# Values of the dilated heads: from four strided token classes per chunk of four heads to copies in class order and one product for all eight

## The chip, the cores and the metric

The kernel runs on one core of one Trainium2 chip, as one launch. The metric is the time on the device in microseconds (us), as the median of several runs. The engines of a core are named as in the profile: PE (TensorE, matrix products) and PEld (its loads of the stationary operand), DVE (VectorE), ACT (ScalarE), POOL (GpSimd), and SP (SyncE), whose queue issues most transfers. They run side by side and wait for one another by semaphores. On-chip memory is SBUF; products are summed in PSUM, eight banks of 512 float32 per partition.

## The reference

One decoder layer on 512 tokens of width 1024, in float32:

```python
x = x + 1/2 * SwiGLU_1(RMSNorm(x))                 # width 2816
h = RMSNorm(x)
[qkv_A | qkv_B | gate_A | gate_B] = h @ W_in       # A: 12 heads of 64, B: 8 heads of 64
y_A = dilated window attention over three groups of four heads:
      (window 128, dilation 1), (512, 4), (2048, 16), merged by their softmax denominators
y_B = block-sparse attention (block 256), causal inside the blocks
x = x + (sigmoid(gate_A) * (y_A @ W_up_A) + sigmoid(gate_B) * (y_B @ W_up_B)) @ W_out
x = x + 1/2 * SwiGLU_2(RMSNorm(x))
return RMSNorm(x)
```

With dilation 4 or 16 a token attends only to tokens of its own class, t % 4. The eight heads of those two groups (heads 4 to 11 of A) are the dilated heads of the title.

## The kernel before

The residual stream is kept transposed, as eight tiles of 128 features by 512 tokens. Every float32 operand is split into two parts, hi and lo; a product is the sum of hi*hi, hi*lo and lo*hi, so `mac` issues three matmuls. After the first feed-forward half, `normed` leaves the normalised stream as `XN[k]`, a pair (hi, lo) of tiles [128, 512] for each k.

All weights come in one stream of tiles [128, up to 1024], in the order of their use: `fetch` loads a tile, `split` casts it to its hi part on ACT and subtracts to get the lo part on DVE (lines 182 and 183), and `weights` hands out the next tile after it has asked for the split of the one after it. The split parts have two buffers each. TensorE's instructions run in the order of the program text; the order of the other engines' is chosen by a planner when the kernel is built.

Queries and keys are projected with the weights as stationary operand and 512 tokens moving (`project`). Then `stacked` scales them by the row factor of the norm (line 460; for the dilated pairs the tokens are put in class order, with strided operands), splits them (462, 463), and sends the parts to their places with transfers on SP's queue (474 and 476). The values have tokens on the partitions: the stationary operand is a tile of 128 tokens of `XN[k]`, and the moving one is 256 columns of weights, the four heads of a chunk c:

```python
mac(ps[t // 2][:, at:at + n], [tokens(x, t, dilated) for x in XN[k]], cols(w, kk, n), ...)
```

For the chunks 1 and 2, which hold the dilated heads, `tokens` takes every fourth token (`by_class(x)[:, t]`), so 128 columns with a step of four elements, 16 bytes. A chunk has 8 x 4 steps of three matmuls, and its four sums of 256 columns share two banks; they are scaled by the row factor as a column per token (`columns`, line 257) into hi and lo parts (506, 507).

The mixers start with the list `FIRST`: pair 0 of heads (before the norm's factor is there), pairs 1 and 2, and chunk 1 of the values. `factors` computes the norm's row factor with a Newton step (230 to 234), `columns` spreads it. After that each of the four dilated heads, and each pair of the other kind, has two parts, scores and weighted sums (`dsa_scores`, `weighted`), and `blend` spreads the steps of the projections named in `BESIDE` over the steps of each part:

```python
FIRST = [("qk", 0), ("qk", 1), ("qk", 2), ("v", 1)]
BESIDE = [
    [("v", 2), ("v", 0)], [("qk", 3)],
```

`project`, `values` and `gate` take turns on four banks ("acc"). In `weighted` the transposed rows go to tiles tagged `pth` and `ptl`, three buffers each. `bias` (line 514) is POOL's only work in the mixers: slopes times distances.

Of the kernel before, what the change touches and what calls it, by code (L numbers as in the profile page):

```python
"""One core: a macaron SwiGLU pair around a gated merge of dilated window attention and MoBA.

The residual stream is kept transposed, [d_model on partitions, tokens], so that every projection
takes the weights as the stationary operand and the tokens as the moving one. A float32 operand is
split exactly into two float32r parts (hi + lo, 12 significant bits each); a product is the sum of
hi*hi, hi*lo and lo*hi, added up in float32 in PSUM. Query-key and probability-value products are
small and carry all four parts, hi and lo stacked on the partitions.

The RMSNorm's row factor is applied to the outputs of the projections that follow it, its gain to
their inputs. With MOBA_TOPK >= the number of blocks every past block is selected, so MoBA is causal  # L10
attention here. The three groups of the dilated attention are one softmax over their joint keys.
"""
# [28 lines left out]
# Heads by pairs, as they are projected: those of the dilated attention, then MoBA's.  # L41
# [3 lines left out]
def by_class(ap):  # L45
    """[P, tokens] as [P, class t % 4, t // 4]."""
    return ap.rearrange("p (i r) -> p r i", r=NT)


def slopes(n):  # L50
# [7 lines left out]
# The projections of the mixers: those before the attention, and those beside each part of it  # L58
# (scores and weighted sums of each head of the dilated attention, then of each pair of MoBA's).
FIRST = [("qk", 0), ("qk", 1), ("qk", 2), ("v", 1)]  # L60
BESIDE = [
    [("v", 2), ("v", 0)], [("qk", 3)],
# [11 lines left out]
def blend(main, side, lead=0):  # L74
    """Run a generator beside others: `lead` steps of the others, then the rest spread over those of `main`.

    Each comes with its number of steps."""
    (main, total), left = main, sum(n for _, n in side) - lead
    steps = (None for g, _ in side for _ in g)
    done = 0  # L80
    for _ in range(lead):
        next(steps, None)
    for at in range(1, total + 1):
        while done * total < left * at:
            next(steps, None)
            done += 1
        next(main, None)
    for _ in main:
        pass
    for _ in steps:  # L90
        pass
# [3 lines left out]
def decoder_layer(ctx: ExitStack, tc: tile.TileContext, xT, gains, gus, gu1, dn1, wqk, wv, wg, wup, wout, gu2, dn2, base, out):  # L95
# [20 lines left out]
    def warm_up(n):  # L116
        """Keep the tensor engine's clock up while it waits."""
        ps = bank("all")
        for _ in range(n):
            nc.tensor.matmul(ps[:, :P], ones, ones, start=True, stop=True)  # L120

# [11 lines left out]
    CHUNKS = [slice(c * P, min(c + 8, FT) * P) for c in range(0, FT, 8)]  # L133

    def mixer_tiles(what, n, *js):
        src = {"qk": lambda j: wqk[2 * n + j], "v": lambda j: wv[n, j], "g": lambda j: wg[2 * n + j]}[what]
        return [((what, n, j), src(j)) for j in js or range(2)]
# [49 lines left out]
    def weights(*key):  # L187
        """The next tile of the stream, split, with the ones after it on their way."""
# [7 lines left out]
    def mac(ps, w, x, first, last):  # L196
        """ps += w.T @ x for split operands."""
# [12 lines left out]
    def normed(i, k):  # L210
        """Tile k of the stream times the gain, split; and its part of the sum of squares."""
# [16 lines left out]
    def newton(y, z, a, out):  # L228
        """out = 1/sqrt(a): a step from the reciprocal of the table's square root."""
# [6 lines left out]
    def factors(i, ps):  # L236
        """1/rms of each token, as rows on all partitions."""
# [14 lines left out]
    def columns(row, dilated):  # L252
        """The same as columns [token of the tile, tile], tiles of 128 tokens or of a class of tokens."""
# [7 lines left out]
    def tokens(x, t, dilated):  # L261
        """Tile t of the tokens of x [P, tokens]."""
        return by_class(x)[:, t] if dilated else x[:, t * P:(t + 1) * P]

# [1 line left out]
    def first_tiles():  # L266
        """Gate and up of the first two tiles, side by side over k as x comes in."""
# [60 lines left out]
    def last_tile(A):  # L328
        """The last tile of the stream in two halves of the tokens, each followed by its part of the output."""
# [99 lines left out]
    with ExitStack() as mix:  # L429
# [15 lines left out]
        def project(t, j, which="acc"):  # L445
            """Queries (j = 0) or keys (j = 1) of a pair of heads, transposed."""
# [6 lines left out]
        def stacked(t, j, ps):  # L453
            v = tpool.tile([P, S], F32, name="qkv", tag="ssq", bufs=1)
            # The scores are kept with the sign turned, as their minimum is then the softmax's bias.
# [8 lines left out]
            # For each head: q as [hi; lo], k as [hi; hi] and [lo; lo].  # L464
# [21 lines left out]
        def values(c):  # L486
            """Values of four heads, tokens on partitions, [hi | lo] per head."""
            # Two tiles of tokens share a bank: its first product clears it for both.
            ps = [bank("acc") for _ in range(2)]
            n = 4 * HD  # L490
            dilated = c in (1, 2)
            col = R["col"][dilated]
            for half in range(2):
                w = weights("v", c, half)
                for kk in range(4):
                    k = 4 * half + kk
                    for t in range(NT):
                        at = (t % 2) * n
                        mac(ps[t // 2][:, at:at + n], [tokens(x, t, dilated) for x in XN[k]], cols(w, kk, n),
                            k == 0 and t % 2 == 0, k == KT - 1 and t % 2 == 1)  # L500
                        yield
            for t in range(NT):
                v = V[t, c] = mp.tile([P, 4 * P], F32R, name=f"v{t}_{c}", tag=f"v{t}_{c % 3}", bufs=1)
                heads = v.rearrange("p (h c) -> p h c", c=P)
                pv = ps[t // 2][:, (t % 2) * n:(t % 2 + 1) * n].rearrange("p (h c) -> p h c", c=HD)
                nc.scalar.mul(heads[:, :, :HD], pv, col[:, t:t + 1])
                nc.vector.scalar_tensor_tensor(heads[:, :, HD:], pv, col[:, t:t + 1], f32(heads[:, :, :HD]),
                                               ALU.mult, ALU.subtract)

        def bias(tag, n, *parts):  # L510
            """Slopes times distances, in [P, n]."""
# [5 lines left out]
        def row_of(row, ps, b, low, den):  # L517
            """exp(score - max) of a row of scores, with its turned maximum and its sum."""
# [3 lines left out]
        def dsa_scores(h, rows):  # L522
            """Rows of the joint softmax of head h of each of the three groups.

            The dilated groups go by the classes t % 4 of the tokens, in which all their keys lie."""
            bb = bias("biasb", 256, (BAND, sl_a[h], 0))
            bd = bias("biasd", 256, (DILATED[:, :P], sl_a[4 + h], 0), (DILATED[:, P:], sl_a[8 + h], P))
            # [low or sum, own or other, by tiles or by classes, tile]
# [5 lines left out]
            for r in range(NT):  # L534
# [5 lines left out]
                # The two parts of the keys side by side: one long product instead of two short ones.  # L540
# [13 lines left out]
            # Each order of the tokens gets the other's minima and sums: a permutation, exact as it adds zeros.  # L554
# [32 lines left out]
        def moba_scores(heads, rows):  # L587
            """Rows of the softmax of each head over all keys up to its own."""
# [16 lines left out]
        def weighted(steps, ytile, half, classes=False):  # L605
            """The rows' sums of values, transposed, into half a tile of y.

            A step is up to four blocks of the rows to transpose, and the products that they go into:
# [266 lines left out]
```

## Time and profile before

| what | us |
|---|---|
| median of 3 runs | 1162.74 |
| lowest and highest run | 1161.46, 1162.74 |
| span of the profiled execution | 1162.7 |
| PE busy | 1150.9 (99%) |
| DVE, ACT, POOL busy | 597.9, 413.5, 19.6 |

The profiled execution's time is its span, from the first to the last instruction; it stands at the median of the runs. Busy times are sums over the span. Matmuls are pipelined and a record of one lasts longer than its place in the stream, so a busy PE is not a PE at its peak: the distance from one start to the next tells the pace. The mean granted clock of PE is 0.999 of full speed.

### The profile page before, as it was taken

To read this page: it belongs to the slowest core of one execution; us is meant where nothing else is said; L and a number is where in the kernel's file an instruction comes from. 1 tells how busy PE (TensorE), PEld (TensorE's weight loads), DVE (VectorE), ACT (ScalarE), POOL (GpSimd) and SP (SyncE) were. 2 spreads that over 40 slices of the span, in tenths; PEclk is the share of its full clock that TensorE was granted. 3 is DMA by queue.
4 is the path that set the end of the run, shared out by engine and by line. 5 is a ranking of instruction groups with operands and counts; after the bars stand their busy time and mean duration, and the time that the engine had idled before them with its cause. 6 is when DMAs were issued, how large, how long until landed. Compare 5 with 4: busy or idle time off the path is not lost.

```text
span 1162.7 us, 13714 instructions
## 1 busy us (share of the span) xinstructions
PE 1150.9 (99%) x5418; PEld 966.8 (83%) x5418; DVE 597.9 (51%) x975; ACT 413.5 (36%) x641; POOL 19.6 (2%) x35
## 2 busy tenths in 40 slices
PE   8999999999999999999999999999999999999997
PEld 7888888888888899888998888888888888888886
DVE  5745444433333633777677667754744444433223
ACT  5433233222222323544454445433422323322222
POOL 0000000000000100000000000000000000000001
PEclk9999999999999999999999999999999999999999
DMA  5232232233233461446364222332233233233321
GB/s 200 93 107 91 95 105 91 94 97 100 87 99 122 140 173 55 128 127 164 111 162 127 74 64 82 110 99 99 91 96 104 91 96 103 91 100 84 98 82 73
DMA packets 37599, 122.14 MB, mean 105 GB/s; under 512 B 4752, under 2 KB 4768, under 8 KB 37536
## 3 DMA queue, kind: packets, MB, share of 16 engines
q1 hardware_dynamic: 37072, 120.08, 34.3%
q10 hardware_dynamic: 432, 1.18, 0.3%
q8 instruction: 42, 0.69, 0.2%
q14 instruction: 21, 0.17, 0.0%
q0 software_dynamic: 32, 0.02, 0.0%
HBM read 103.44 MB, written 2.10 MB: 91 GB/s over the span
## 4 chain that ended last, share of the span: by engine, by line
PE 98%; DVE 0%; DMA 0%; ACT 0%; issue 0%; DVEq 0%; POOLq 0%
PE ps_all L199 20%; PE ps_all L201 20%; PE ps_all L200 20%; PE ps_acc L199 9%; PE ps_acc L201 9%; PE ps_acc L200 9%; PE ps_all L276 2%; PE ps_out L640 2%; PE ps_att L621 1%; PE ps_att L199 1%; PE ps_att L200 1%; PE ps_att L201 1%; PE ps_att L596 1%; DMA g_sb<-in_gains_dram 0%; PE ps_att L538 0%; PE ps_att L550 0%
## 5 line engine op out<-in xcount | busy, mean ns | idle before, releaser
L182 ACT CAST whi<-raw 128x1024 fp32r<-128x1024 f32 (+2 forms) x201 | 202.8, 1010 | 562.4 <-PE ps_all L200 259.9
L183 DVE TENSOR_TENSOR wlo<-raw,whi 128x1024 fp32r<-128x1024 f32 (+2 forms) x202 | 236.2, 1170 | 174.1 <-ACT whi L182 174.0
L200 PE MATMUL ps_all<-xl,whi 128*128 128x512 f32 x672 | 261.4, 389 | 0.0
L199 PE MATMUL ps_all<-xh,whi 128*128 128x512 f32 x672 | 261.4, 389 | 0.0
L201 PE MATMUL ps_all<-xh,wlo 128*128 128x512 f32 x672 | 261.4, 389 | 0.0
L200 PEld LDWEIGHTS ps_all<-xl,whi 128*128 128x128 f32 x672 | 126.1, 188 | 26.3
L201 PEld LDWEIGHTS ps_all<-xh,wlo 128*128 128x128 f32 x672 | 126.1, 188 | 26.3
L199 PEld LDWEIGHTS ps_all<-xh,whi 128*128 128x128 f32 x672 | 126.1, 188 | 26.0
L199 PE MATMUL ps_all<-ah,whi 128*128 128x512 f32 (+1 forms) x374 | 143.1, 383 | 0.0
L200 PE MATMUL ps_all<-al,whi 128*128 128x512 f32 (+1 forms) x374 | 142.7, 382 | 0.0
L201 PE MATMUL ps_all<-ah,wlo 128*128 128x512 f32 (+1 forms) x374 | 142.7, 382 | 0.0
L199 PE MATMUL ps_acc<-xh,whi 128*128 128x512 f32 x272 | 110.2, 405 | 0.0
L201 PE MATMUL ps_acc<-xh,wlo 128*128 128x512 f32 x272 | 106.9, 393 | 0.0
L200 PE MATMUL ps_acc<-xl,whi 128*128 128x512 f32 x272 | 106.4, 391 | 0.0
L290 DVE TENSOR_TENSOR fu<-ps_all,rrow 128x512 f32<-128x512 f32 x44 | 30.4, 691 | 124.1 <-PE ps_all L201 124.1
L200 PEld LDWEIGHTS ps_all<-al,whi 128*128 128x128 f32 x374 | 70.2, 188 | 15.2
L201 PEld LDWEIGHTS ps_all<-ah,wlo 128*128 128x128 f32 x374 | 70.2, 188 | 15.1
L199 PEld LDWEIGHTS ps_all<-ah,whi 128*128 128x128 f32 x374 | 70.2, 188 | 15.0
L288 DVE TENSOR_TENSOR fg<-ps_all,rrow 128x512 f32<-128x512 f32 x44 | 30.4, 691 | 79.8 <-PE ps_all L201 79.7
L201 PEld LDWEIGHTS ps_acc<-xh,wlo 128*128 128x128 f32 x272 | 51.0, 188 | 11.3
L200 PEld LDWEIGHTS ps_acc<-xl,whi 128*128 128x128 f32 x272 | 51.3, 189 | 7.4
L199 PEld LDWEIGHTS ps_acc<-xh,whi 128*128 128x128 f32 x272 | 51.3, 188 | 7.4
(158 smaller groups left out, 1321.3 us busy)
## 6 DMA issues: line engine op xcount, KB each, us to landing
raw<-in_gu_dram SPq DMA_DIRECT2D x84, 512.0 KB, 3.4
raw<-in_dn_dram SPq DMA_DIRECT2D x32, 512.0 KB, 3.5
raw<-in_wqk_dram SPq DMA_DIRECT2D x20, 512.0 KB, 3.5
ks<-qkhl SPq DMA_DIRECT2D x40, 256.0 KB, 4.9
raw<-in_wg_dram SPq DMA_DIRECT2D x16, 512.0 KB, 3.5
raw<-in_dn_dram SPq DMA_DIRECT2D x16, 384.0 KB, 3.1
raw<-in_wv_dram SPq DMA_DIRECT2D x10, 512.0 KB, 4.0
qs<-qkhl SPq DMA_DIRECT2D x40, 128.0 KB, 2.6
```

Of the source, the lines that this page charges most:

```text
L182: nc.scalar.copy(hi[:, s], raw[:, s])
L183: nc.vector.tensor_tensor(lo[:, s], raw[:, s], f32(hi[:, s]), ALU.subtract)
L199: nc.tensor.matmul(ps, wh, xh, start=first, stop=False)
L200: nc.tensor.matmul(ps, wh, xl, start=False, stop=False)
L201: nc.tensor.matmul(ps, wl, xh, start=False, stop=last)
L276: nc.tensor.matmul(ps[j], w[:, at:at + P], x, start=k == 0 and n == 0, stop=k == KT - 1 and n == 2)
L288: nc.vector.tensor_tensor(g, ps[0], R, ALU.mult)
L290: nc.vector.tensor_tensor(u, ps[1], R, ALU.mult)
L596: nc.tensor.matmul(ps[:, :n], Q[NA + h][:, i * P:(i + 1) * P], K[NA + h][:, part, :n], start=part == 0, stop=part == 1)
L621: nc.tensor.transpose(pt[:, n * P:(n + 1) * P], block, ident)
L640: nc.tensor.matmul(to(po), V[v[0], v[1] // 4][:, v[1] % 4 * P:(v[1] % 4 + 1) * P], x[:, first:first + n], start=done == 1, stop=done == 2 ...
```

## The change

The values of the eight dilated heads are no longer two chunks of four. A new part `("vd", 0)` stands right after pair 0 in `FIRST`, and `("v", 1)` and `("v", 2)` are gone from the lists. `values_by_class` takes all four "acc" banks, one for each class of tokens, and works through the eight tiles of the stream. For each, POOL copies the hi and the lo part into class order, into tiles that share the tags `pth` and `ptl` (three buffers each); the products take 128 consecutive columns of a copy as stationary operand and all eight heads' 512 columns of weights as the moving one. The weights are four tiles of two times 512 columns in place of two times two tiles of four times 256. The eviction is the same per class and chunk (`keep_values`). Comments and documentation strings are removed too.

```diff
-FIRST = [("qk", 0), ("qk", 1), ("qk", 2), ("v", 1)]
+FIRST = [("qk", 0), ("vd", 0), ("qk", 1), ("qk", 2)]
 BESIDE = [
-    [("v", 2), ("v", 0)], [("qk", 3)],
+    [("v", 0)], [("qk", 3)],
...
     def mixer_tiles(what, n, *js):
-        src = {"qk": lambda j: wqk[2 * n + j], "v": lambda j: wv[n, j], "g": lambda j: wg[2 * n + j]}[what]
-        return [((what, n, j), src(j)) for j in js or range(2)]
+        src = {"qk": lambda j: wqk[2 * n + j], "v": lambda j: wv[max(0, n - 2), j], "vd": lambda j: wvd[j], "g": lambda j: wg[2 * n + j]}[what]
+        return [((what, n, j), src(j)) for j in js or range(4 if what == "vd" else 2)]
...
         def values(c):
             ps = [bank("acc") for _ in range(2)]
             n = 4 * HD
-            dilated = c in (1, 2)
-            col = R["col"][dilated]
...
-                        mac(ps[t // 2][:, at:at + n], [tokens(x, t, dilated) for x in XN[k]], cols(w, kk, n),
+                        mac(ps[t // 2][:, at:at + n], [x[:, t * P:(t + 1) * P] for x in XN[k]], cols(w, kk, n),
...
+                keep_values(t, c, ps[t // 2][:, (t % 2) * n:(t % 2 + 1) * n], R["col"][False])
+
+        def keep_values(t, c, pv, col):
+            v = V[t, c] = mp.tile([P, 4 * P], F32R, name=f"v{t}_{c}", tag=f"v{t}_{c % 3}", bufs=1)
+            heads = v.rearrange("p (h c) -> p h c", c=P)
+            pv = pv.rearrange("p (h c) -> p h c", c=HD)
+            nc.scalar.mul(heads[:, :, :HD], pv, col[:, t:t + 1])
+            nc.vector.scalar_tensor_tensor(heads[:, :, HD:], pv, col[:, t:t + 1], f32(heads[:, :, :HD]),
+                                           ALU.mult, ALU.subtract)
+
+        def values_by_class():
+            ps = [bank("acc") for _ in range(NT)]
+            n = 8 * HD
+            for quarter in range(4):
+                w = weights("vd", 0, quarter)
+                for kk in range(2):
+                    k = 2 * quarter + kk
+                    copies = []
+                    for x, tag in zip(XN[k], ("pth", "ptl")):
+                        xc = mp2.tile([P, S], F32R, name="xc", tag=tag, bufs=3)
+                        nc.gpsimd.tensor_copy(xc.rearrange("p (r i) -> p r i", r=NT), by_class(x))
+                        copies.append(xc)
+                    for r in range(NT):
+                        mac(ps[r], [x[:, r * P:(r + 1) * P] for x in copies], cols(w, kk, n), k == 0, k == KT - 1)
+                        yield
+            for r in range(NT):
+                for c in (1, 2):
+                    keep_values(r, c, ps[r][:, (c - 1) * 4 * HD:c * 4 * HD], R["col"][True])
...
+            if what == "vd":
+                return values_by_class(), NT * KT
...
-        "wv": np.stack([_moving(v[:, c:c + 256], 4) for c in range(0, v.shape[1], 256)]),
+        "wv": np.stack([_moving(v[:, c:c + 256], 4) for c in (0, 768, 1024)]),
+        "wvd": _moving(v[:, 256:768], 2),
```

## Rows read from the trace of the kernel before

**Rows 1.** The page: busy time of each engine; chain that ended last.

```profile
PE 1150.9 (99%) x5418; PEld 966.8 (83%) x5418; DVE 597.9 (51%) x975; ACT 413.5 (36%) x641; POOL 19.6 (2%) x35
...
PE 98%; DVE 0%; DMA 0%; ACT 0%; issue 0%; DVEq 0%; POOLq 0%
```

**Rows 2.** Windows: stretch, its length, busy time (x instructions) of each engine.

```profile
372.92:384.26 11.34, 11.34 (x51) 9.39 (x50) 5.12 (x6) 4.28 (x6) 4.04 (x8) 1.00 0.54 182
384.26:406.03 21.77, 21.77 (x98) 18.07 (x96) 17.95 (x32) 7.35 (x9) 0.00 (x0) 1.00 0.52 145
406.03:452.30 46.27, 46.27 (x206) 46.27 (x206) 15.38 (x31) 12.69 (x25) 0.60 (x2) 1.00 0.46 125
```

**Rows 3.** Weight loads by form, 406 to 431 us, dilated values: total, mean.

```profile
L199 PEld LDWEIGHTS ps_acc<-whi,xh 128*128 128x128 f32 x37 | 12.2, 328 | 0.0
```

**Rows 4.** The same from 452.3 to 464 us, plain values.

```profile
L199 PEld LDWEIGHTS ps_acc<-whi,xh 128*128 128x128 f32 x32 | 6.1, 192 | 0.0
```

**Rows 5.** Timeline, TensorE, dilated and plain products: start, duration, engine.

```profile
407.08 0.39 PE L201 MATMUL ps_acc<-whi,xl 128*128 128x256 f32 x1
407.32 0.39 PE L199 MATMUL ps_acc<-whi,xh 128*128 128x256 f32 x1
...
453.70 0.28 PE L200 MATMUL ps_acc<-wlo,xh 128*128 128x256 f32 x1
453.82 0.28 PE L201 MATMUL ps_acc<-whi,xl 128*128 128x256 f32 x1
```

**Rows 6.** POOL's groups by form over the span.

```profile
L514 POOL TENSOR_SCALAR bias<-consts 128x256 f32<-128x256 f32 x4 | 1.6, 406 | 390.8 <-PE ps_att L201 375.5 <-DVE st L519 15.2
...
L371 POOL TENSOR_TENSOR yo<-yo,rrow 128x256 f32<-128x256 f32 x8 | 5.6, 729 | 499.0 <-ACT rrow L363 499.0
```

**Rows 7.** Timeline, 591 to 595 us, POOL and VectorE.

```profile
591.23 0.62 POOL L514 TENSOR_SCALAR bias<-consts 128x512 f32<-128x512 f32 x1 [100.61 <-DVE low L519]
...
593.11 1.23 DVE L183 TENSOR_TENSOR wlo<-raw,whi 128x1024 fp32r<-128x1024 f32 x1
...
593.26 1.55 POOL L514 TENSOR_SCALAR bias<-consts 128x512 f32<-128x512 f32 x1 [1.42 <-DVE low L519]
...
594.25 1.10 DVE L463 TENSOR_TENSOR qkhl<-qkv,qkhl 128x512 fp32r<-128x512 f32 x1
```

**Rows 8.** Timeline of VectorE, 387 to 400 us.

```profile
387.19 3.35 DVE L231 RECIPROCAL root<-root 128x512 f32<-128x512 f32 x1 [0.90 <-ACT root L230]
390.58 0.69 DVE L232 SCALAR_TENSOR_TENSOR step<-root 128x512 f32<-128x512 f32 x1
...
394.40 0.69 DVE L460 SCALAR_TENSOR_TENSOR qkv<-ps_att,rrow 128x512 f32<-128x512 f32 x1
...
397.76 1.23 DVE L183 TENSOR_TENSOR wlo<-raw,whi 128x1024 fp32r<-128x1024 f32 x1
398.89 0.70 DVE L463 TENSOR_TENSOR qkhl<-qkv,qkhl 128x512 fp32r<-128x512 f32 x1
399.62 1.05 DVE L460 SCALAR_TENSOR_TENSOR qkv<-ps_acc,rrow 128x512 f32<-128x512 f32 x1
```

**Rows 9.** Timeline, keys 409 to 417, first head 468 to 472 us.

```profile
409.04 3.15 SPq L476 DMA_DIRECT2D ks<-qkhl  x4
...
415.97 0.62 ACT L462 CAST qkhl<-qkv 128x512 fp32r<-128x512 f32 x1 [4.44 <-DMA ks<-qkhl]
...
468.74 2.13 DVE L585 TENSOR_SCALAR prow<-prow,jf 128x128 f32<-128x128 f32 x8
...
471.50 0.60 PE L621 MATMUL ps_att<-ident,prow 128*128 128x128 f32 x4
```

**Rows 10.** Timeline of TensorE at the start.

```profile
7.12 2.08 PE L276 MATMUL ps_all<-xh,whi 128*128 128x512 f32 x4 [2.28 <-ACT xh L215]
8.99 1.91 PE L276 MATMUL ps_all<-xh,wlo 128*128 128x512 f32 x4
10.70 1.91 PE L276 MATMUL ps_all<-xl,whi 128*128 128x512 f32 x4
```

More of the change, by code (lines that the diff above doesn't have):

```diff
@@ L94, in decoder_layer @@
 @with_exitstack
-def decoder_layer(ctx: ExitStack, tc: tile.TileContext, xT, gains, gus, gu1, dn1, wqk, wv, wg, wup, wout, gu2, dn2, base, out):
+def decoder_layer(ctx: ExitStack, tc: tile.TileContext, xT, gains, gus, gu1, dn1, wqk, wv, wvd, wg, wup, wout, gu2, dn2, base, out):
     nc = tc.nc
@@ L502, in values @@
             for t in range(NT):
[L503 to L508, printed above, removed]
+                keep_values(t, c, ps[t // 2][:, (t % 2) * n:(t % 2 + 1) * n], R["col"][False])
[24 more added lines that the diff above has]
+                    keep_values(r, c, ps[r][:, (c - 1) * 4 * HD:c * 4 * HD], R["col"][True])
         def bias(tag, n, *parts):
```

## The prediction, made before the changed kernel was run

> **What bounds the kernel now.** I read the page's busy shares and its chain first, then the chain's stages by windows, and inside the stage that the diff touches the weight loads, the start times of the products and the other engines' queues. TensorE is the bound throughout: it is busy 99% of the span and is 98% of the chain that ended last [rows 1]. So a change is worth what it takes out of TensorE's stream, less whatever TensorE must newly wait for.
>
> The windows cut the start of the mixers into the first pair of heads (from 372.92), the pairs 1 and 2 (from 384.26), and the dilated values with twelve score products among them (from 406.03) [rows 2]. In the second of these, 96 products of 512 columns (x98 with the two cut at the edges) take 21.77 us: 0.227 us each. In the third, 192 products of only 256 columns and the twelve scores take 46.27 us, and the weight loads are busy for all of it, not 83% as in the stage before: there the loads set the pace, not the products. The loads that take every fourth token as stationary column are 328 ns [rows 3]; the same loads for the undilated values are 192 ns [rows 4]. The starts agree: 0.24 us from one dilated product to the next, 0.12 us from one plain product to the next, both with 256 columns [rows 5].
>
> **The change, part by part.**
>
> *Removed.* The projections v1 and v2 with their 2 x 32 x 3 = 192 products: 46.27 us [rows 2] less the twelve scores, at the 0.12 us of an unstrided product of 256 columns [rows 5] 1.4 us, is 44.9 us, 0.234 us each.
>
> *Added on TensorE.* Four classes x eight tiles x three parts = 96 products of 512 columns on a stationary tile without a stride. A load of 192 ns hides behind a product of 0.227 us, as it does in the stage of rows 2, so the price is that row's 21.8 us. The net is -23.1 us. If the load stayed at 328 ns it would be 31.5 us; a stationary operand of the same shape without a stride is what rows 4 show, so I leave that out of the range.
>
> *Added on POOL.* Sixteen copies of 128x512, two for each tile of the stream, read with a step of four elements. POOL is otherwise nearly idle. No row shows it read with a step. Without one, and with one operand, it takes 0.41 us for 256 elements [rows 6] and 0.62 us for 512 (the slopes at 591.23 [rows 7]): 0.20 us fixed and 0.82 ns an element. What a step costs others: VectorE's 128x512 scaling rises from 0.69 to 1.05 us when its operands go by classes, 0.70 ns an element [rows 8]; TensorE's load rises by (328 - 192)/128 = 1.06 ns [rows 3, 4]. That puts a copy at 0.98 to 1.17 us; I take 1.1, of which 0.9 is reading. Bounds: 0.62 us if the step is free; and the two-operand POOL row, 0.73 us for 256 elements or 2.1 ns each [rows 6], with 1.06 ns more for the step, gives 1.8 us.
>
> *Do the copies themselves come in time?* Each pair serves 12 products, 2.72 us. Three pairs have room. They can start when the first feed-forward half has let go of its memory, near 373, and the first is wanted at 384.3; six copies (6.6 us), the eight slopes (4.0 us) and all of VectorE's work there (5.1 us) [rows 2] still end by 389, when the third pair is wanted at 389.7. The other ten start at 387.0, when the first pair is read, and the last must be there at 384.3 + 7 x 2.72 = 403.3: at up to 1.6 us a copy that holds if nothing disturbs POOL.
>
> *What disturbs it, and what it disturbs.* The slopes at 593.26 took 1.55 us instead of 0.62, while VectorE subtracted two SBUF operands (593.11 to 594.34); VectorE's next subtraction of two operands then took 1.10 us [rows 7], and 0.70 where POOL is idle [rows 8]. So POOL and a VectorE instruction with two SBUF operands take turns. VectorE has such a train just here: from 390.58 to 398.99 it steps Newton's root, splits a tile of weights, takes eight columns, splits the first queries, scales twice (from PSUM, one SBUF operand) and splits the next tile of weights [rows 8], 8.4 us with no gap worth naming. That last split is wanted when the fourth tile of the new projection begins, at 384.3 + 3 x 5.44 = 400.6; before it has 1.6 us to spare. Now the eight copies of the last four pairs fall into the train. Taking turns it ends at 390.58 + 8.4 + 8 x 0.9 - 1.2 (the two scalings run beside the copies) = 405.0, and TensorE waits 4.4 us for weights. Behind the train stand the evictions of the new sums; they are not late, as the columns come before the split. With copies of 0.62 us (0.42 of reading) the wait is 0.6 us; with 1.8 us (1.6) it is 10.0 us.
>
> A rule that speaks against the change: the Trainium skill, GPSIMD Engine Reference, section Performance pitfalls for Q7 kernels, gives 2.9 cycles an element at 1.2 GHz where the step is over 8 bytes, and 1.9 below. Rows 6 and 7 show 0.82 ns an element without a step, half of the page's lower figure, and no row here has the step. By the page a copy would be an estimated 0.20 + 1.24 = 1.44 us, the wait 7.1 us and the time 1146.7 us, where by the rows it is 4.4 us and 1144.0 us.
>
> *Evictions.* The same 16 instructions in place of 2 x 8; the next projection takes the first of the four banks at once, but that bank is closed nine products (2.0 us) before the end, and its two scalings on ScalarE and two subtractions on VectorE, half as long as the 0.70 us of 128x512 [rows 8] or a little more, overlap to about three in a row. I put 0, at most 1 us.
>
> *Order.* Between the keys of pair 1 and the first scores lay pair 2 and v1, now only pair 2, 10.9 us and three steps of v0, 1.1 us. The keys' way is the scaling 1.05, a cast 0.62, a subtraction 0.70 and the transfers, 6.9 us from issue at 409.04 to the cast that waited for them until 415.97 [rows 8, 9]: 9.5 us with the gaps, inside 12.0. The first head's scores now have v0 alone beside them, 96 products at 0.12 over 13 steps, so 0.9 us of TensorE a step, and not another 96 at 0.234; the second head has as much from its gate, 48 products of 512 columns. The rows of the first head are ready at 470.87 and transposed at 471.50 [rows 9], with v0 beside them then too; 0.6 us to spare, so 0 with up to 1 us lost.
>
> *Sum.* The profiled execution's span is 1162.7 us, and the median of the runs is 1162.74, so nothing is added for what lies around it. 1162.7 - 44.9 + 21.8 + 4.4 = **1144.0 us**.
>
> **The rivals.**
> - *Hidden* (1139 to 1141.5): copies near 0.7 us, or the split put ahead of the columns in VectorE's queue. For it: 1.6 us of slack and three buffers. Against it: rows 7 and the order of rows 8. 1139.6 us.
> - *Slow copies* (1146.5 to 1152.5): 1.4 to 1.8 us each, by the two-operand row; 7 to 10 us of waits: 1147 to 1150.
> - *The clock falls.* At the start TensorE idled 2.28 us, and its next eight products took 1.71 to 1.87 us for four, 0.43 us each, twice the later 0.227, as 1.2 GHz stands to 2.4 [rows 10]. If a wait of 4.4 us in one piece does the same, at least eight products cost 1.8 us more: 1146 us. The granted clock is 1.00 in every window of rows 2, as there is no wait in them. The Trainium skill, TensorE: Matmul & The Clock Gate, Part 1, says that an idle engine is throttled to 1.2 GHz; by it the wait would cost that much on top, if it is not broken up by work.
> - *Slower than before*: POOL's copies set the pace of the whole projection. The place is the wait of each group of products for its pair; the price is 8 x reading - 2.8, and it decides when a copy passes 3.4 us (8 x 3.2 - 2.8 = 22.8). The only row that slow per element is VectorE's reciprocal, 3.35 us for 512 and no copy; POOL's slowest row is a third of it. At 3.8 us: 1165.6 us.
> - *No change*: the loads keep their 328 ns and the wait comes on top: 1162.7 - 44.9 + 31.5 + 4.4 = 1153.7 us, still faster; only with slow copies does it reach 1160 or more. Rows 4 speak against it.
>
> **How the numbers follow.** The forecast (1141.5 to 1146.5, without a fall of the clock) has 45%, hidden copies 25%, slow copies 17%, a fallen clock 8%, slower 3%, no change 2%. A difference of 0.2%, 2.3 us, is about what these runs can tell from none. Faster 0.95, within 0.2% 0.02, slower 0.03. The range runs from 1139.0, all hidden and every small term nought, to 1152.5, copies of 1.8 us with the clock's price on top.
>
> **What would show it.** Right: no weight load of 328 ns is left; 96 products of 512 columns start 0.227 us apart except where they wait; POOL has sixteen copies of about 1.1 us, longer beside VectorE's subtractions; the longest wait of TensorE in the new projection is near its fourth tile of weights and names VectorE's split (or its copy). Wrong, if that wait is nil, if the waits stand at each pair of copies, if the loads of the copied tiles are not near 192 ns, or if the first scores wait for keys.

## The result, and the profile after

| | before | after |
|---|---|---|
| median of the runs, us | 1162.74 | 1145.30 (1144.41 to 1146.97, 4 runs) |
| ratio, 95% interval | | 0.9852 [0.9841, 0.9864] |
| span of the profiled execution, us | 1162.7 | 1144.1 |

The forecast was 1144.0 us within 1139.0 to 1152.5. Of all executions behind this text one, of 3176.71 us in the experiment e3 below, was disturbed and stands in no number. The page of the changed kernel, first the busy times, then the shares of the chain that ended last:

```profile
PE 1129.3 (99%) x5322; PEld 939.9 (82%) x5322; DVE 605.0 (53%) x975; ACT 413.0 (36%) x641; POOL 42.5 (4%) x51
...
PE 97%; DVE 2%; DMA 0%; issue 0%; ACT 0%; DVEq 0%; POOLq 0%
```

Beside [rows 1], TensorE has 96 products fewer, POOL sixteen instructions more and 23 us more of busy time, and VectorE now has 2% of the chain, where it had 0%. These 2% hold the longest wait of the new stage. The windows of the first pair and of the new projection (length, then busy time and instructions of PE, PEld, DVE, ACT and POOL, granted clock, share of the DMA engines, GB/s), and of two stretches near the projection's end:

```profile
371.63:382.98 11.35, 11.35 (x51) 9.38 (x50) 7.90 (x6) 4.19 (x6) 10.75 (x10) 1.00 0.52 169
382.98:410.64 27.66, 24.59 (x98) 18.95 (x96) 22.33 (x33) 8.72 (x14) 16.08 (x15) 0.94 0.43 122
403.40:405.00 1.60, 1.60 (x4) 1.31 (x5) 1.60 (x2) 0.33 (x1) 0.00 (x0) 0.50 0.49 142
407.00:408.00 1.00, 1.00 (x6) 0.77 (x6) 0.00 (x0) 0.00 (x0) 0.00 (x0) 1.00 1.03 254
```

The eight heads' values take 27.66 us, where the two chunks before took about 45 [rows 2]. TensorE is idle for 3.07 us of them, and for another 3 us it runs at a granted clock of 0.50. Its waits from 370 to 440 us (total, times, longest) and its weight loads in the projection:

```profile
PE ps_acc L200 <- DVE wlo L183: 2.8, 1, 2.8
PE ps_acc L199 <- DVE v L509: 0.2, 1, 0.2
```

```profile
L199 PEld LDWEIGHTS ps_acc<-whi,xc 128*128 128x128 f32 x31 | 6.2, 201 | 2.1 <-POOL xc L525 0.5
```

There is one wait worth naming, it is for VectorE's split, and the loads of the copied tiles are 201 ns and not 328 [rows 3]. TensorE's timeline at the fourth tile of weights, and after the last product (start, duration):

```profile
399.55 0.39 PE L201 MATMUL ps_acc<-whi,xc 128*128 128x512 f32 x1
400.01 0.47 PE L199 MATMUL ps_acc<-whi,xc 128*128 128x512 f32 x1
403.32 0.79 PE L200 MATMUL ps_acc<-wlo,xc 128*128 128x512 f32 x1 [2.83 <-DVE wlo L183]
403.91 0.63 PE L201 MATMUL ps_acc<-whi,xc 128*128 128x512 f32 x1
404.33 0.63 PE L199 MATMUL ps_acc<-whi,xc 128*128 128x512 f32 x1
...
406.81 0.39 PE L199 MATMUL ps_acc<-whi,xc 128*128 128x512 f32 x1
...
410.08 0.39 PE L201 MATMUL ps_acc<-whi,xc 128*128 128x512 f32 x1
410.64 0.47 PE L199 MATMUL ps_acc<-xh,whi 128*128 128x512 f32 x1 [0.17 <-DVE v L509]
```

Products start 0.23 us apart. The first product of the fourth tile needs only the hi part (`whi`) and starts 0.23 late; the second needs the lo part and starts 3.31 us after it, 3.08 late. Then products come 0.43 us apart: the eight starts from 403.32 to 406.81 take 3.49 us instead of 8 x 0.233 = 1.86, so 1.6 us go to the clock. The next projection starts 0.33 us late, for a bank. Together: 96 x 0.233 = 22.4, and 0.23 + 3.08 + 1.6 + 0.33, makes 27.6 of the 27.66 us.

The queue of VectorE before that split, and POOL's copies beside it:

```profile
389.30 1.05 DVE L232 SCALAR_TENSOR_TENSOR step<-root 128x512 f32<-128x512 f32 x1
390.38 1.47 DVE L233 TENSOR_TENSOR step<-step,mean 128x512 f32<-128x512 f32 x1
391.78 2.13 DVE L183 TENSOR_TENSOR wlo<-raw,whi 128x1024 fp32r<-128x1024 f32 x1
393.83 1.58 DVE L234 SCALAR_TENSOR_TENSOR rrow<-step,root 128x512 f32<-128x512 f32 x1
...
398.68 1.22 DVE L257 CUSTOM_DVE_ANT_0 rest<-rrow,ident 128x128 f32<-128x128 f32 x1
399.83 0.28 DVE L257 CUSTOM_DVE_ANT_0 rest<-rrow,ident 128x128 f32<-128x128 f32 x1
...
402.06 1.21 DVE L183 TENSOR_TENSOR wlo<-raw,whi 128x1024 fp32r<-128x1024 f32 x1
```

```profile
388.68 1.12 POOL L525 CAST xc<-xh 128x512 fp32r<-128x512 f32 x1 [0.38 <-PE ps_acc L200]
389.74 1.56 POOL L525 CAST xc<-xl 128x512 fp32r<-128x512 f32 x1
...
392.77 2.10 POOL L525 CAST xc<-xl 128x512 fp32r<-128x512 f32 x1
...
398.54 1.19 POOL L525 CAST xc<-xl 128x512 fp32r<-128x512 f32 x1
```

The train runs from 389.30 to the split's end at 403.27, 13.97 us, where it had 8.4 before [rows 8]. The split of the third tile took 2.13 us instead of 1.22, the Newton step on line 234 1.58 instead of 0.68. The copies stop at 399.73, and from there on VectorE's column takes 0.28 us, where the one before took 1.22. POOL stretches with it: 1.10 to 1.12 us for a copy beside VectorE's reciprocal, which reads one operand, and up to 2.10 beside its split of two SBUF operands.

ScalarE shows a second link that the forecast did not have:

```profile
398.30 0.62 ACT L462 CAST qkhl<-qkv 128x512 fp32r<-128x512 f32 x1 [8.41 <-DVE qkv L460]
398.82 1.04 ACT L182 CAST whi<-raw 128x1024 fp32r<-128x1024 f32 x1
```

The cast that makes the fourth tile's hi part stands in ScalarE's queue behind pair 0's cast, and that one waited 8.41 us for VectorE's scaling. So both parts of the fourth tile came late out of the same train.

### The profile page after: what moved, and what is told of

Same layout as the page of the kernel before. It is cut to its first block, busy times and chain, and to the rows that moved or that the text cites. A ratio compares the mean times of both kernels' runs of the same rounds, so it can differ in the third digit from the quotient of the medians.

```text
span 1144.1 us, 13562 instructions
## 1 busy us (share of the span) xinstructions
PE 1129.3 (99%) x5322; PEld 939.9 (82%) x5322; DVE 605.0 (53%) x975; ACT 413.0 (36%) x641; POOL 42.5 (4%) x51
## 4 chain that ended last, share of the span: by engine, by line
PE 97%; DVE 2%; DMA 0%; issue 0%; ACT 0%; DVEq 0%; POOLq 0%
PE ps_all L199 21%; PE ps_all L200 21%; PE ps_all L201 20%; PE ps_acc L199 8%; PE ps_acc L200 8%; PE ps_acc L201 8%; PE ps_all L276 2%; PE ps_out L664 2%; PE ps_att L645 1%; PE ps_att L201 1%; PE ps_att L199 1%; PE ps_att L200 1%; PE ps_att L620 1%; DMA g_sb<-in_gains_dram 0%; DVE rest L257 0%; PE ps_att L562 0%
```

## The experiments

Two theories were put to the test. **Turns**: the 3 us and the clock behind them come from POOL's copies and VectorE's train taking turns; the gain itself from fewer and cheaper weight loads. **Order**: the gain comes from where the projection stands, or the wait is there whoever makes the copies. Some expectations name a third, **POOL's rate**: the copies themselves come too slowly for TensorE. It can be set aside at once, as in none of the traces does a product of the projection wait for a copy. And one question that the prediction had answered from a duration alone: are the copies needed at all? Each run is given with its ratio to the kernel before on the same chip.

| run | what | median, us | ratio, 95% interval |
|---|---|---|---|
| e1 | eight heads in one product, no copies | 1141.49 | 0.9819 [0.9804, 0.9833] |
| e2 | copies, products of 256 columns | 1147.13 | 0.9869 [0.9852, 0.9885] |
| e3 | copies on ScalarE | 1145.33 (3 runs) | 0.9849 [0.9830, 0.9867] |
| e4 | projection last in `FIRST` | 1150.12 | 0.9891 [0.9876, 0.9906] |
| e5 | POOL's copies without a step | 1140.64 | 0.9813 [0.9796, 0.9829] |
| e6 | columns and pair 0 later in the program | 1146.77 | 0.9865 [0.9850, 0.9879] |
| e7 | the split put ahead of them in the queue | 1144.29 | 0.9846 [0.9831, 0.9861] |
| e8 | e1, last in `FIRST` | 1147.99 | 0.9878 [0.9864, 0.9893] |
| e9 | no copies, 256 columns: place alone | 1162.69 | 0.9996 [0.9987, 1.0006] |
| e10 | the changed kernel again | 1146.77 | 0.9863 [0.9849, 0.9878] |
| e11 | e1 again, beside e10 | 1141.48 | 0.9815 [0.9800, 0.9829] |

**e1: no copies.** The copy loop is taken out, and the products read the stream with its step:

```diff
-                        mac(ps[r], [x[:, r * P:(r + 1) * P] for x in copies], cols(w, kk, n), k == 0, k == KT - 1)
+                        mac(ps[r], [tokens(x, r, True) for x in XN[k]], cols(w, kk, n), k == 0, k == KT - 1)
```

> The eight heads in one product of 512 columns, but without copies: the stationary tiles keep their step of four elements, POOL does nothing new. What it tells apart is which half of the change takes the 23 us out. If a load with a step costs its 328 ns each time (as the prediction counted for the rival of no change), 96 of them take 31.5 us and there is no wait of VectorE's, as POOL is idle: 1162.7 - 44.9 + 31.5 = 1149 us, and the copies are what brings the gain. If the loads with a step can follow one another at the 0.234 us that the starts of the dilated products showed before, they hide almost wholly behind products of 0.227 us: 96 x 0.234 = 22.5 us and 1140.3 us, better than the changed kernel by 5 us, and the copies are not needed.

1141.49 us: faster than the changed kernel, and 1.2 us above the second of the two expected times. TensorE's weight loads and products in the middle of the stage:

```profile
394.88 0.31 PEld L200 LDWEIGHTS ps_acc<-wlo,xh 128*128 128x128 f32 x1
395.12 0.31 PEld L201 LDWEIGHTS ps_acc<-whi,xl 128*128 128x128 f32 x1
```

```profile
395.11 0.40 PE L200 MATMUL ps_acc<-wlo,xh 128*128 128x512 f32 x1
395.35 0.39 PE L201 MATMUL ps_acc<-whi,xl 128*128 128x512 f32 x1
```

A load with the step lasts 0.31 us, yet the next one starts 0.24 us after it (0.235 on average): two loads overlap. The products of 512 columns start 0.235 us apart, where those on plain tiles start 0.233 apart. The stage, from its first product to the start of its last, takes 405.22 - 382.89 = 22.33 us; in the changed kernel 410.08 - 382.99 = 27.09.

**e2: copies, but two products of 256 columns** for each product of 512.

```diff
-                        mac(ps[r], [x[:, r * P:(r + 1) * P] for x in copies], cols(w, kk, n), k == 0, k == KT - 1)
+                        xr = [x[:, r * P:(r + 1) * P] for x in copies]
+                        wk = cols(w, kk, n)
+                        for c in range(2):
+                            half = slice(c * n // 2, (c + 1) * n // 2)
+                            mac(ps[r][:, half], xr, [x[:, half] for x in wk], k == 0 and c == 0, k == KT - 1 and c == 1)
```

> The copies stay, but each tile of a copy moves two times 256 columns, as two products of four heads: 192 products. If the plain loads of 192 ns follow at the 0.118 us of the plain values before, 192 x 0.118 = 22.7 us on TensorE, within 1 us of the changed kernel (1145 to 1146 us): then taking eight heads at once is worth nothing beside the copies. If the loads set a pace of 0.19 us, 36.9 us: 1160 us.

1147.13 us, 1.1 us above what was expected of the first case, and far from the 1160 us of the second. Twice as many products start 0.12 us apart, each on a plain tile, and the wait at the fourth tile is there again, with 0.50 of the clock from 404.5 to 407.4 us behind it:

```profile
389.96 0.28 PE L200 MATMUL ps_acc<-wlo,xc 128*128 128x256 f32 x1
390.08 0.28 PE L201 MATMUL ps_acc<-whi,xc 128*128 128x256 f32 x1
...
403.72 0.39 PE L200 MATMUL ps_acc<-wlo,xc 128*128 128x256 f32 x1 [2.98 <-DVE wlo L183]
```

So the copies alone bring nearly all of what the change brought, and the wider product alone (e1) brings more than the change. Either one lifts the bound of the weight loads; these runs show no second bound of that kind for the other to lift.

**e3: the copies on ScalarE.**

```diff
-                        nc.gpsimd.tensor_copy(xc.rearrange("p (r i) -> p r i", r=NT), by_class(x))
+                        nc.scalar.copy(xc.rearrange("p (r i) -> p r i", r=NT), by_class(x))
```

> The same copies, order and products, but ScalarE makes the copies instead of POOL. Theory (turns): what TensorE waits for in the changed kernel is VectorE's split of the fourth tile, late because VectorE's two-operand instructions take turns with POOL's copies. ScalarE takes no turns with VectorE: VectorE's train is as short as before, 8.4 us, the wait of 3.3 us and the fall of the clock are gone, 1140 to 1142 us, unless ScalarE's sixteen copies of 0.7 to 1.1 us hold up its own casts of the weights. Rival (any copy is too much in this place): the wait stays at 3 us or more wherever the copies run: 1145 us or more.

The runs took 1142.93, 1145.33 and 1145.67 us, above the expected 1140 to 1142, and e3 as a whole can't be told from the change. The profile is of the first, at a mean granted clock of 0.999; the other two, at 0.996 and 0.997, left no trace. In the profile the projection's only wait is the 0.2 us for a bank at its end, and its first to last start are 22.17 us. VectorE's train, from its first instruction to the split of the fourth tile, takes 8.44 us, as short as before the change:

```profile
390.24 0.69 DVE L232 SCALAR_TENSOR_TENSOR step<-root 128x512 f32<-128x512 f32 x1
...
397.48 1.20 DVE L183 TENSOR_TENSOR wlo<-raw,whi 128x1024 fp32r<-128x1024 f32 x1
```

The wait went elsewhere. ScalarE's timeline, then TensorE's, before the projection:

```profile
374.83 1.11 ACT L525 CAST xc<-xh 128x512 fp32r<-128x512 f32 x1
375.83 0.72 ACT L215 ACTIVATE xh<-x,g_sb 128x512 fp32r<-128x512 f32 x1
```

```profile
376.61 0.49 PE L199 MATMUL ps_att<-xh,whi 128*128 128x512 f32 x1 [1.77 <-ACT xh L215]
377.43 0.50 PE L200 MATMUL ps_att<-xl,whi 128*128 128x512 f32 x1 [0.33 <-DVE xl L216]
```

Copies of the same length on another engine (1.09 to 1.13 us) leave VectorE's train alone: that is what the turns predict. But five of them came ahead of the hi part of the stream's last tile, and pair 0 waited 2.1 us for its two parts.

**e4 and e8: the projection last.** `FIRST` has pairs 1 and 2 ahead of the values; e8 has no copies either.

```diff
-FIRST = [("qk", 0), ("vd", 0), ("qk", 1), ("qk", 2)]
+FIRST = [("qk", 0), ("qk", 1), ("qk", 2), ("vd", 0)]
```

> The same values by class, but after pairs 1 and 2 instead of before them. Theory (turns): the wait of 3.3 us in the changed kernel stands before the fourth tile of weights, as VectorE's train of two-operand instructions, which spreads the norm's factor, takes turns with POOL's copies. In the later place the train is over before the last ten copies run: no wait for a split, no fall of the clock, about 5 us less than the changed kernel, 1140 to 1141 us. Rival (POOL's rate): the copies themselves are too slow for TensorE; then waits of the same size stay, at the copies, and the time stays at 1144 to 1146 us.

> Eight heads in one product without copies, as in the best run so far, but after pairs 1 and 2. In the run with the copies in this place TensorE waited twice, 2.7 and 1.9 us, for the scalings of pair 2's queries and keys, which read the banks that the new values want; the casts behind them waited for transfers of keys. If that is so and the copies have no part in it, the same two waits and the fall of the clock are here without any copy: 1141.5 + 2.7 + 1.9 + about 2 = 1147 to 1149 us. If the copies made those waits, the time is that of the early place, 1141 to 1142 us.

Both are slower than in front: 1150.12 us with copies, 1147.99 without, 6.5 us more than e1. What was expected of e8 came; what was expected of e4 did not, neither the 1140 to 1141 us of the turns nor the 1144 to 1146 of POOL's rate. No wait for a split is left in e4, as the turns have it, but two others are there, of 2.73 and 1.88 us, which neither theory had. TensorE in e8, with no POOL copies in it, and ScalarE in e4:

```profile
408.95 0.60 PE L199 MATMUL ps_acc<-whi,xh 128*128 128x512 f32 x1 [2.88 <-DVE qkv L460]
411.77 0.78 PE L199 MATMUL ps_acc<-whi,xh 128*128 128x512 f32 x1 [1.75 <-DVE qkv L460]
...
412.78 0.63 PE L201 MATMUL ps_acc<-whi,xl 128*128 128x512 f32 x1
413.21 0.63 PE L199 MATMUL ps_acc<-whi,xh 128*128 128x512 f32 x1
```

```profile
406.56 0.62 ACT L462 CAST qkhl<-qkv 128x512 fp32r<-128x512 f32 x1 [5.40 <-DMA ks<-qkhl]
```

The projection wants all four banks at once. Here the sums of the pairs just before it still stand in them: they are let go by the scaling on line 460, which waits for the casts, which wait for the transfers of keys to free their tiles. The waits again cost clock too: from 412 to 417 us the products are 0.43 us apart. In front, after pair 0 (whose sums stand in other banks), nothing of that kind is in the way. So "done first" matters once the projection takes four banks. By itself it brings nothing, as e9 shows.

**e5: POOL's copies without the step.** The copy takes the tokens in their own order, so the values belong to other tokens.

```diff
-                        nc.gpsimd.tensor_copy(xc.rearrange("p (r i) -> p r i", r=NT), by_class(x))
+                        nc.gpsimd.tensor_copy(xc, x)
```

> POOL's sixteen copies stay, but read without the step: the tokens are copied in their own order, so the values of the dilated heads belong to other tokens than they should, and the rest of the work is the same. Theory (turns): a copy takes 0.62 us, of which 0.42 is reading; the train ends 8 x 0.5 = 4 us earlier than with 0.9 us of reading, so the wait at the fourth tile falls from 3.3 us to under 1 us, and the clock does not fall: 1140 to 1142 us. Rival (the wait hangs on the number of copies, as each costs VectorE a turn): the wait stays above 2 us and the clock falls: 1144 us or more.

1140.64 us, with no wait but the bank's 0.2, and a mean granted clock of 0.999. POOL's copies in the middle of the stage:

```profile
388.41 0.62 POOL L525 CAST xc<-xh 128x512 fp32r<-128x512 f32 x1 [1.63 <-PE ps_acc L200]
...
391.21 1.25 POOL L525 CAST xc<-xh 128x512 fp32r<-128x512 f32 x1 [1.62 <-PE ps_acc L200]
392.41 1.07 POOL L525 CAST xc<-xl 128x512 fp32r<-128x512 f32 x1
```

With the step gone, the copy is 0.62 us alone, as the prediction's lower bound had it, and 1.07 to 1.25 beside VectorE's two-operand instructions. Everything else is the changed kernel; VectorE's train takes 10.07 us instead of 13.97. The 4.7 us between the two medians, measured at different times, are the waits and the clock; the changed kernel's own timeline gave 0.23 + 3.08 + 1.6 = 4.9.

**e6 and e7: the train itself.** e6 moves the undilated columns and the scaling of pair 0 behind the projection in the program; e7, shown here, also ties them behind the split of the fourth tile of weights with `issue_after`.

```diff
-                nc.vector.tensor_tensor(lo[:, s], raw[:, s], f32(hi[:, s]), ALU.subtract)
+                state["lo", stream[t][0]] = nc.vector.tensor_tensor(lo[:, s], raw[:, s], f32(hi[:, s]), ALU.subtract).ins
...
-        R["col"] = [columns(R["row"], dilated) for dilated in (False, True)]
-        for j in range(2):
-            stacked(0, j, early[j])
-        for item in FIRST[1:]:
+        R["col"] = [None, columns(R["row"], True)]
+        for n, item in enumerate(FIRST[1:]):
             for _ in part(*item)[0]:
                 pass
+            if n == 0:
+                with tc.issue_after(state["lo", ("vd", 0, 3)]):
+                    R["col"][0] = columns(R["row"], False)
+                    for j in range(2):
+                        stacked(0, j, early[j])
```

> The place of the values stays, but the four undilated columns and the scaling and splitting of pair 0 come behind them in the program, so that VectorE's train before the split of the fourth tile is shorter by four columns of 0.3 us, two scalings of 0.7 and one split of 0.7 us. Theory (turns): the split ends 3 to 4 us earlier, the wait of 3.3 us falls under 1 us and the clock does not fall: 1140 to 1142 us. Rival (POOL's rate): TensorE waits for the last copies instead, 1144 to 1146 us.

> The same as the run with the shorter train, whose edit the planner undid, but now the undilated columns and the scaling and splitting of pair 0 are tied behind the fourth tile's split in VectorE's queue. Theory (turns, and what stands ahead of the split): between the row factor and the split only the four dilated columns are left, the split ends near 401 us in the trace and not at 403.3, TensorE waits under 1 us, the clock does not fall: 1140.5 to 1142.5 us, with POOL's copies at full length. Rival (POOL's rate): TensorE then waits for the last copies, 2 us or more, and the time stays at 1144 us or above.

In e6 the planner put VectorE's instructions back into the order they had; the split starts at 402.15 and the wait is 2.84 us, so the run tells nothing of the theories, and its 1146.77 us are those of the changed kernel (e10). In e7 the order did change. VectorE's queue, then TensorE:

```profile
399.72 1.07 DVE L257 CUSTOM_DVE_ANT_0 rest<-rrow,ident 128x128 f32<-128x128 f32 x1
...
400.72 1.21 DVE L183 TENSOR_TENSOR wlo<-raw,whi 128x1024 fp32r<-128x1024 f32 x1
```

```profile
401.99 0.50 PE L200 MATMUL ps_acc<-wlo,xc 128*128 128x512 f32 x1 [0.89 <-DVE wlo L183]
402.33 0.40 PE L201 MATMUL ps_acc<-whi,xc 128*128 128x512 f32 x1
402.56 0.39 PE L199 MATMUL ps_acc<-whi,xc 128*128 128x512 f32 x1
...
409.38 0.47 PE L199 MATMUL ps_acc<-xh,whi 128*128 128x512 f32 x1 [1.77 <-DVE v L509]
```

The wait for the split falls from 2.83 to 0.89 us, and the products after it are at full pace: no clock was lost. But what was pushed behind the split now stands ahead of the evictions, and the next projection waits 1.77 us for its bank. The four columns left ahead of the split take 0.98 to 1.07 us each, beside a copy each, where one alone takes 0.28. A copy made a VectorE instruction on two SBUF operands longer by up to about 0.9 us whatever its own size: in the changed kernel 0.28 became 1.22, 0.68 became 1.58, and 1.22 became 2.13. At 1144.29 us the run can't be told from the change by its interval, and the expected 1140.5 to 1142.5 us were missed.

**e9: the place and the layout of the weights alone.** No copies, and two products of 256 columns, that is the old work in the new place.

```diff
-                        mac(ps[r], [x[:, r * P:(r + 1) * P] for x in copies], cols(w, kk, n), k == 0, k == KT - 1)
+                        xr = [tokens(x, r, True) for x in XN[k]]
+                        wk = cols(w, kk, n)
+                        for c in range(2):
+                            half = slice(c * n // 2, (c + 1) * n // 2)
+                            mac(ps[r][:, half], xr, [x[:, half] for x in wk], k == 0 and c == 0, k == KT - 1 and c == 1)
```

> Neither copies nor eight heads in one product: only the place and the weights' layout of the changed kernel stay, with 192 products of 256 columns on stationary tiles with a step. If the gain lies in how many loads with a step there are, and a load's pace of 0.234 us is all that counts, this is as slow as the kernel before: 192 x 0.234 = 44.9 us, 1162 to 1163.5 us. If doing the values first is worth something by itself, it is faster by that; more than 3 us would be against the reading that the halved number of loads made the gain.

1162.69 us over ten runs, ratio 0.9996 [0.9987, 1.0006]: nothing. Its weight loads (count, total and mean) and a window inside the stage and just behind it:

```profile
L199 PEld LDWEIGHTS ps_acc<-whi,xh 128*128 128x128 f32 x64 | 21.0, 329 | 0.0
```

```profile
382.00:432.00 50.00, 50.00 (x216) 49.07 (x216) 20.14 (x38) 11.55 (x17) 0.00 (x0) 1.00 0.26 77
```

TensorE never waits, and its loads are busy for 49.07 of 50 us: the bound of [rows 2], in another place. The order theory falls.

**e10 and e11: the changed kernel and e1 once more**, on one chip.

> The changed kernel itself on the same chip as the next one, for a direct comparison: 1144.5 to 1146.5 us.

> The eight heads in one product without copies, beside the changed kernel on the same chip: 1140.5 to 1142.5 us, 3 to 5 us less than the changed kernel, which would be what its copies cost (3.1 us of wait and 1.4 us of the lower clock, less 0.9 us as loads with a step leave 0.235 and not 0.227 us between products). If the difference of the two earlier runs came from their chips, the two are within 1.5 us here.

1146.77 us with the copies, 1141.48 without. The intervals, [0.9849, 0.9878] and [0.9800, 0.9829], stand clear of each other: leaving the copies out is worth 5.3 us here, a little more than the 3 to 5 that were expected. The spans of the two profiles differ by 4.7 us; the trace of e10 has the same wait of 2.83 us for the same split, and after it products 0.43 us apart, where e11 has neither.

## Why the prediction was right

**Removed.** Forecast 44.9 us. The span fell by 18.6 us, of which 1.3 had gone before the mixers began (the first product of pair 0 starts at 371.63, not at 372.92 as in [rows 2]); 17.3 are left, and the medians differ by 17.4. The new stage took 27.66 us, so what went away was about 45.0. One reading under the sum does not hold: that the span of the profiled execution stands at the median of the runs. In every execution that has both on record, the time is 1.7 to 2.7 us longer than the span (1145.84 and 1144.1 for the profile of the changed kernel). So the trace of the kernel before is one of a longer execution. The sum stays good, because 1162.74 is a measured median.

**Added on TensorE.** Forecast 21.8 us for 96 products. The two runs without a wait in the stage (e3, e5) take 22.17 us over 95 starts, 22.4 for 96: 0.233 us each and not 0.227. Low by 0.6. The trace of the kernel before has both paces: 0.227 in the stage that the forecast read, and 0.234 in the last products of the feed-forward half, from 368.71 to 372.92 us. What decides between them no run tells.

**The copy.** Forecast 1.1 us, measured 1.10 to 1.12 where VectorE takes no turns with it, and 0.62 without the step (e5), the bound given for that. With the prediction's fixed 0.20 us, the copy costs (1.10 - 0.20)/512 = 1.76 ns an element. The Trainium skill, GPSIMD Engine Reference, Performance pitfalls for Q7 kernels, states that a step over 8 bytes makes a POOL read dearer; the traces agree with that, and not with its size: 2.1 cycles at 1.2 GHz here, instead of its 2.9, and the measurement decides.

**The wait.** Forecast 4.4 us at the split of the fourth tile, from a train of 8.4 + 8 x 0.9 - 1.2 = 14.4 us. The train took 13.97, and TensorE stood for 0.23 + 3.08 = 3.3 us. Place, engine and cause are as predicted. It is 1.1 us shorter since the train ran 0.4 faster and the products before it 0.5 slower, and since one product of the tile (0.23 us) can go before the lo part is there. That the turns are its cause is shown by three runs: copies without the step (e5), copies on another engine (e3), no copies (e1). In all three this wait is gone. What the forecast did not have is that the hi part came late as well, by 0.23 us, through ScalarE's queue.

**The clock.** The forecast left it out and gave it 8% as a rival, at 1.8 us. It happened: granted clock 0.50, or 1.2 GHz, between 403.4 and 406.5, 1.6 us; and again in e2, e6 and e10, behind the same wait. The forecast's 26.2 us for the stage (21.8 + 4.4) became 22.4 + 3.3 + 0.33 + 1.6 = 27.6. The excess of 1.4 us is the 1.3 by which 1144.0 fell short of 1145.3, and without the clock there would be none. So what came is the rival and not the case of 45%, which was stated without a fall of the clock, though 1145.30 lies between its bounds. That the total came out near is luck in part: the wait was taken 1.1 us too long, and the clock, 1.6 us, was left out. The waits of 1.77 us in the traces of e3 and e7 did not bring the clock down. The Trainium skill, TensorE: Matmul & The Clock Gate, Part 1, states that an idle engine is throttled to 1.2 GHz; the trace agrees for this wait, of 3.1 us.

**The hidden case** was priced at 1139.6 us; e5, which is that case made by hand, gave 1140.64. **Evictions, keys and head 0**: the bank cost 0.33 us where 0 to 1 was allowed. No wait for keys or for the first head's scores appears: from 440 us on, TensorE's only waits are 1.2 and 1.0 us at the last norm, as in the kernel before.

**The step that failed** was one in *Added on TensorE* and again in the rival *No change*: "If the load stayed at 328 ns it would be 31.5 us". That took a duration for a pace. Loads with the step overlap; [rows 5] had them 0.24 us apart while [rows 3] had them 328 ns long, and 192 x 0.234 = 44.9 had been worked out from the pace one paragraph earlier. Rightly priced, 96 strided loads cost 96 x 0.235 = 22.6 us, 0.2 more than plain ones, and *No change* would have been 1162.7 - 44.9 + 22.6 = 1140.4 without copies; e1 and e11 gave 1141.5. It did not touch the forecast, but it hid what the runs then showed: the gain can be had by giving each strided load 512 columns to hide behind, and the copies only add the wait. Where it went is in e9 (neither: 1162.7), e2 (copies alone: 1147.1), e1 (width alone: 1141.5) and the change (both: 1145.3). The version without copies is the best of all kernels here that compute the whole layer.

What stays open: why the start of the mixers moves from one trace to the next (369.90 us in e3, 371.36 to 372.92 in the others), and e4's 2.1 us over e8, measured on different chips. The two traces give the copies no price there: their spans, 1147.7 and 1147.3 us, differ by 0.4, of which 0.3 lies ahead of the mixers.

## What to carry to other kernels

Price an operation that is pipelined by the distance between starts, not by the length of its record: 328 ns of load at a pace of 0.235 us all but hides behind a product of 0.233. When weight loads are the bound, first widen what moves past each load; only if that can't be done, pay for copies that make the load cheap. A helper engine that is idle is not free: POOL's copies took turns with VectorE's instructions on two SBUF operands, where ScalarE's did not but held up ScalarE's own work. What counts is the last instruction of the delayed train that TensorE waits for, plus the clock that TensorE loses by waiting.

## What the runs showed of the hardware

- A copy of 128x512 with a step of 16 bytes took 1.10 to 1.12 us on POOL, undisturbed, and 1.09 to 1.13 on ScalarE; POOL took 0.62 without the step.
- POOL's turns with VectorE hold for the short custom instruction on two SBUF operands as well: 0.28 us alone, 0.96 to 1.22 beside a copy, so that in proportion the small ones suffer most. Beside ScalarE's copies VectorE's train took no longer than without any (8.44 us in e3).
- LDWEIGHTS with the step, 0.31 to 0.33 us long, ran 0.235 us apart, behind products of 256 and of 512 columns alike.
- One wait of 3.1 us in TensorE halved its granted clock for about 3 us. In e8 the clock was still 1.00 behind a wait of 2.88 us; behind a second one of 1.75 us, which ended 2.8 us later, it was 0.50 for 5 us.
